# Attention's scores and transpositions over four PSUM banks, its outputs over one

## The chip, the cores and the metric

The kernel runs on one core of one Trainium2 chip, in one launch. The metric is the device time of that launch in microseconds (us): the median of three runs, with the lowest and the highest beside it.

## The reference, cut to what matters

Two layers (DEPTH = 2) of a hybrid mixer over 512 tokens of width 1024. Each layer normalises x, multiplies it with one wide input matrix, runs two branches beside each other and multiplies their concatenation with an output matrix. One branch is a gated linear recurrence (HGRN2, 8 heads of 128). The other, which the change touches, is sliding-window attention with 16 query heads of 64, two key/value heads and a learned sink per head:

```python
def sliding_window_attention(q, k, v, sinks):
    ...
    s = jnp.einsum('bnqkgd,bnskd->bnkgqs', qb, kw).astype(jnp.float32) * ATT_SCALE
    ...
    s = jnp.where(mask[None, :, None, None, :, :], s, NEG_INF)
    ...
    p = jax.nn.softmax(jnp.concatenate([s, sink], axis=-1), axis=-1)[..., :-1]
    o = jnp.einsum('bnkgqs,bnskd->bnqkgd', p.astype(v.dtype), vw)
    return o.reshape(B, S, KV * G * D)
...
    y = jnp.einsum('bse,ed->bsd', jnp.concatenate([o_h, o_a], axis=-1), w_out)
    return x + rms_norm(y, g_post)
```

A query block of 128 sees its own block of keys (up to the diagonal) and the block before it (past the diagonal).

## The kernel before

**The large products.** Every projection is cut into units of one PSUM bank (128 x 512). `step()` issues three matmuls of a unit (all on L284: high by high, high by low, low by high part of float32 operands that were split into two float32r parts); two units take turns. Weights come by DMA into `raw`, ACT casts the high part `whi` (L178) and DVE subtracts to get `wlo` (L179). Finished units are read out of PSUM by ACT or DVE.

**The attention.** `att_stream` (L613) is woven into the projections by `merge`, about one attention piece for a few L284 steps. A layer has 16 attention steps, numbered 0 to 15 here: four groups g of four heads, and for each the four query blocks n. A step with n = 0 sees one key block, the others two. Step i has three pieces on PE, which stand in the stream at different times:

- **S**, the scores (`att_scores`, L530): one bank with 8 matmuls (L541) where n = 0; else two banks with 4 matmuls each (L552). DVE masks them in PSUM (L544, or L556), takes the maximum (L545 or L557) and makes the negated maximum (`negm`, L560). Then ACT reads the bank and takes four exponentials (L566, two for each bank where there are two), POOL divides by the sum (L573). A score bank is free when its last exponential has been read.
- **T**, the transposition of the probabilities (`att_transpose`, L576), two steps later: one bank, 4 transposes (L579). ACT casts it (L330), DVE subtracts (L331), and the bank is free; POOL then masks the two halves (L591).
- **U**, the output (`att_value`, L598), four steps later: one bank, 2 or 4 matmuls of 128x512 (L605). ACT copies its upper half to the tile `u` (L607), of which there is one buffer; DVE adds the halves into `oa` in two instructions (L611), and the bank is free.

**The banks.** PSUM has 8 banks. Three are the units' (`pj`). Three, `sc0` to `sc2`, turn through `sc()`: scores, transpositions, and in other stages the norms' transpositions and the recurrence's products. Two are `ac`, taken in turn for U and, after the attention, for two products of the recurrence (L768, L779).

**What sets the order.** PE takes its instructions in program order, and so do DVE, ACT and POOL. The matmuls of attention and recurrence are pinned to the order in which they are written; a scheduler places everything else around them by its own model of times, and puts a wait in front of the instruction that needs a bank which is still being read. An instruction that waits on PE holds back all that stand behind it.

Of the kernel before, what the change touches and what calls it, by code (L numbers as in the profile page):

```python
# [10 lines left out]
F32 = mybir.dt.float32  # L11
# [29 lines left out]
PJ, SC = 3, 3  # L41
# [28 lines left out]
def hybrid_kernel(ctx: ExitStack, tc: tile.TileContext, x, wkv, win, wout, g_pre, g_post, lbp, ghead, sinks,  # L70
                  gcol_c, cos_f, sin_f, cos_t, sin_t, masks_c, out):
    nc = tc.nc
    P = 128
# [6 lines left out]
    ps = ctx.enter_context(tc.tile_pool(name="ps", bufs=2, space=bass.MemoryType.PSUM))  # L80
    dr = ctx.enter_context(tc.tile_pool(name="dr", bufs=1, space=bass.MemoryType.DRAM))

    def pin(ins):
        return tc.keep_in_program_order(ins)
# [2 lines left out]
        return ps.tile([P, 512], F32, tag="pj", name="pj", bufs=PJ)  # L87

    sc_tiles = [ps.tile([P, 512], F32, tag=f"sc{i}", name=f"sc{i}", bufs=1) for i in range(SC)]
    sc_turn = [0]  # L90

    def sc():
        sc_turn[0] += 1
        return sc_tiles[sc_turn[0] % SC]

    def ac():
        return ps.tile([P, 512], F32, tag="ac", name="ac", bufs=8 - PJ - SC)

    def tmp(tag, dt=F32, n=1):

        t = tp.tile([P, n, 512] if n > 1 else [P, 512], dt, tag=tag, name=tag, bufs=TB[tag])
        return t
# [25 lines left out]
    for l in range(1, DEPTH):  # L128
        i = plan_order.index((l, "kv"))
# [199 lines left out]
    def split_psum(hi, lo, src):  # L329
        nc.scalar.copy(hi, src)  # L330
        nc.vector.tensor_tensor(lo, src, hi.bitcast(F32), op=ALU.subtract)  # L331
# [96 lines left out]
    def layer(l, last):  # L428
# [101 lines left out]
        def att_scores(g, n):  # L530
            v = g // 2
            q = qs[g]
            hs = slice(4 * g, 4 * g + 4)
            t_ = slice(n * P, (n + 1) * P)
            mx_ = sm.tile([P, 4], F32, tag="mx", name="mx")
            cur = []
            if n == 0:
                S = sc()
                for h in range(4):
                    for p in range(2):  # L540
                        pin(nc.tensor.matmul(S[:, h * P:(h + 1) * P], lhsT=q[:, h, t_], rhs=kst[v][p][:, 0:P],  # L541
                                         start=(h == 0 and p == 0), stop=(h == 3 and p == 1)))
                Sv = S.rearrange("p (h s) -> p h s", h=4)
                nc.vector.copy_predicated(Sv, am4, neg.unsqueeze(2).broadcast_to([P, 4, P]))  # L544
                nc.vector.tensor_reduce(mx_, Sv, axis=AX.X, op=ALU.max)  # L545
                cur = [Sv[:, h, :] for h in range(4)]
            else:
                for hp_ in range(2):
                    S = sc()
                    for h in range(2):  # L550
                        for p in range(2):
                            pin(nc.tensor.matmul(S[:, h * 256:(h + 1) * 256], lhsT=q[:, 2 * hp_ + h, t_],  # L552
                                             rhs=kst[v][p][:, (n - 1) * P:(n + 1) * P],
                                             start=(h == 0 and p == 0), stop=(h == 1 and p == 1)))
                    Sv = S.rearrange("p (h s) -> p h s", h=2)
                    nc.vector.copy_predicated(Sv[:, :, P:2 * P], am2, Sv[:, :, 0:P])  # L556
                    nc.vector.tensor_reduce(mx_[:, 2 * hp_:2 * hp_ + 2], Sv[:, :, P:2 * P], axis=AX.X, op=ALU.max)  # L557
                    cur += [Sv[:, h, P:2 * P] for h in range(2)]
            negm = sm.tile([P, 4], F32, tag="negm", name="negm")
            nc.vector.scalar_tensor_tensor(negm, mx_, -SCALE, nsnk[:, l, hs], op0=ALU.mult, op1=ALU.min)  # L560
            ds_ = sm.tile([P, 4], F32, tag="ds", name="ds")
            nc.vector.tensor_tensor(ds_, snk[:, l, hs], negm, op=ALU.add)
            pt = tmp("s")
            sums = sm.tile([P, 4], F32, tag="sums", name="sums")
            for h in range(4):
                nc.scalar.activation(pt[:, h * P:(h + 1) * P], cur[h], AF.Exp, bias=negm[:, h:h + 1], scale=SCALE,  # L566
                                     accum_out=sums[:, h:h + 1])
            es = sm.tile([P, 4], F32, tag="es", name="es")
            nc.scalar.activation(es, ds_, AF.Exp)
            nc.vector.tensor_tensor(sums, sums, es, op=ALU.add)  # L570
            nc.vector.reciprocal(sums, sums)
            pv = pt.rearrange("p (h s) -> p h s", h=4)
            nc.gpsimd.tensor_tensor(pv, pv, sums.unsqueeze(2).broadcast_to([P, 4, P]), op=ALU.mult)  # L573
            return pt

        def att_transpose(g, n, pt, odd):  # L576
            T = sc()
            for h in range(4):
                pin(nc.tensor.transpose(T[:, h * P:(h + 1) * P], pt[:, h * P:(h + 1) * P], ident))  # L579
            tt_ = tmp("a", F32R, 2)  # L580
            split_psum(tt_[:, 0], tt_[:, 1], T)
            if n == 0:
                return [(n, tt_[:, 0]), (n, tt_[:, 1])]
            terms = []
            for which in range(2):
                if which == 0:
                    d = big.tile([P, 2, 512], F32R, tag="oy", name="pcur", bufs=6) if odd else tmp("b", F32R, 2)
                else:
                    d = big.tile([P, 2, 512], F32R, tag="q", name="pprev", bufs=QB)
                sg = -1 if which == 0 else 1  # L590
                nc.gpsimd.affine_select(out=d.rearrange("p a (h t) -> p (a h) t", h=4),  # L591
                                        in_=tt_.bitcast(F32).rearrange("p a (h t) -> p (a h) t", h=4),
                                        pattern=[[0, 8], [-sg, P]], compare_op=ALU.is_ge, fill=0.0,
                                        base=-which, channel_multiplier=sg)
                terms += [(n - which, d[:, 0]), (n - which, d[:, 1])]
            return terms

        def att_value(g, n, terms):  # L598
            v = g // 2
            t_ = slice(n * P, (n + 1) * P)  # L600
            if g == len(oa):
                oa.append(big.tile([P, 2, 512], F32, tag="oy", name="oa", bufs=6))
            U = ac()
            for i, (blk, d) in enumerate(terms):
                pin(nc.tensor.matmul(U, lhsT=vst[v][:, blk, :], rhs=d, start=(i == 0), stop=(i == len(terms) - 1)))  # L605
            ul = tmp("u")
            nc.scalar.copy(ul[0:64, :], U[64:128, :])  # L607
            Uv = U.rearrange("p (a b t) -> p a b t", a=2, b=2)
            lv = ul.rearrange("p (a b t) -> p a b t", a=2, b=2)
            for b in range(2):  # L610
                nc.vector.tensor_tensor(oa[g][64 * b:64 * b + 64, :, t_], Uv[0:64, :, b, :], lv[0:64, :, b, :], op=ALU.add)  # L611
# [60 lines left out]
        def hgrn(a):  # L672
# [94 lines left out]
            for j, f, k, q, A in hs:  # L767
                SU = ac()  # L768
                for n in range(NT - 1):
                    pin(nc.tensor.matmul(SU[:, n * P:(n + 1) * P], lhsT=kps[j][:, n * P:(n + 1) * P], rhs=vs(j, n), start=True, stop=True))  # L770
                st = sm.tile([P, 3, P], F32, tag="st", name="st", bufs=2)
                nc.scalar.copy(st[:, 0], SU[:, 0:P])
                for n in range(1, NT - 1):
                    nc.vector.scalar_tensor_tensor(st[:, n], st[:, n - 1], tots[j][:, n:n + 1], SU[:, n * P:(n + 1) * P],
                                                   op0=ALU.mult, op1=ALU.add)
                sts.append(st)
                yield 1.5
# [38 lines left out]
        def zh_stream(s):  # L816
            def evac(tt, o):
# [9 lines left out]
                def rest():  # L827
                    T = sc()
                    for j in range(4):
                        pin(nc.tensor.transpose(T[:, j * P:(j + 1) * P], g[:, j * P:(j + 1) * P], ident))  # L830
                    Tv = T.rearrange("p (j t) -> p j t", j=4)
                    nc.scalar.activation(hi[:, :, t_], Tv, AF.Copy, scale=gh[:, l:l + 1])
                    nc.vector.scalar_tensor_tensor(lo[:, :, t_], Tv, gh[:, l:l + 1], hi[:, :, t_].bitcast(F32), op0=ALU.mult, op1=ALU.subtract)
# [241 lines left out]
def _tables():  # L1075
# [3 lines left out]
    c, s = np.cos(ang).astype(np.float32), np.sin(ang).astype(np.float32)  # L1079
    cf = np.ascontiguousarray(np.tile(c.T, (4, 1)))  # L1080
    sf = np.ascontiguousarray(np.tile(s.T, (4, 1)))
# [48 lines left out]
```

## Time and profile before

| | before |
|---|---|
| median of 3 runs | 927.55 us |
| lowest, highest | 927.0, 927.8 us |
| the profiled execution's own time | 927.92 us |
| its span, first to last instruction | 926.2 us |
| PE busy | 908.4 us, 98% |
| DVE, ACT, POOL busy | 672.1, 462.5, 268.8 us |
| granted TensorE clock | 0.999 |

A matmul's busy time in the profile runs from its start to its modelled end, and consecutive ones overlap. How long PE really takes for a piece is therefore read from start to start. The attention of layer 0 lies at about 59 to 171 us, that of layer 1 at about 516 to 628 us.

### The profile page before, as it was taken

How to read it: one execution, taken by the hardware profiler on the slowest of the kernel's cores; microseconds unless marked ns; L12 is line 12 of the kernel's file. 1: busy time of each engine (PE TensorE's matmuls, PEld its weight loads, DVE VectorE, ACT ScalarE, POOL GpSimd, SP SyncE). 2: the span in 40 equal slices, each digit the busy share in tenths (PEclk: the TensorE clock that was granted, in tenths of full speed). 3: DMA queues.
4: the chain of work that ended last, by engine and by line, in shares of the span. 5: the costliest groups of instructions: out<-in, count | busy, mean ns of one | idle time of the engine just before them, and what ended most of it. 6: DMA issues, size and time to landing. Idle time of an engine off the chain costs nothing.

```text
span 926.2 us, 18985 instructions
## 1 busy us (share of the span) xinstructions
PE 908.4 (98%) x7240; PEld 751.1 (81%) x7240; DVE 672.1 (73%) x1326; ACT 462.5 (50%) x1100; POOL 268.8 (29%) x286
## 2 busy tenths in 40 slices
PE   8999999999999999999989999999999999999996
PEld 6888887878888888788878878888787887888885
DVE  5968977885766783955786689878867577748556
ACT  5535767536364451444453466674554636325242
POOL 3425443242221311311332254441323203113102
PEclk9999999999999999999999999999999999999999
DMA  6684612322222242423356555122223223323213
GB/s 223 187 234 135 171 36 80 92 82 80 70 86 94 64 136 69 138 70 112 117 160 178 162 148 171 58 69 92 70 80 99 62 81 114 104 70 94 91 35 136
DMA packets 56570, 100.74 MB, mean 109 GB/s; under 512 B 6560, under 2 KB 9120, under 8 KB 56480
## 3 DMA queue, kind: packets, MB, share of 16 engines
q1 hardware_dynamic: 56192, 99.40, 35.8%
q8 instruction: 57, 0.93, 0.4%
q14 instruction: 33, 0.27, 0.1%
q10 hardware_dynamic: 288, 0.14, 0.1%
HBM read 86.93 MB, written 12.58 MB: 107 GB/s over the span
## 4 chain that ended last, share of the span: by engine, by line
PE 85%; DVE 8%; ACT 3%; issue 2%; POOL 1%; DMA 0%; POOLq 0%; DVEq 0%; SPq 0%; ACTq 0%
PE pj L284 71%; PE sc L713 2%; PE sc L552 2%; PE ac L605 2%; DVE wlo L179 2%; PE ac L782 2%; PE ac L785 1%; PE ac L770 1%; ACT s L566 1%; PE sc L579 1%; PE sc L830 1%; DVE mx L557 1%; POOL r L345 1%; DVE a L331 1%; PE sc L760 1%
## 5 line engine op out<-in xcount | busy, mean ns | idle before, releaser
L284 PE MATMUL pj<-hhi,wlo 128*128 128x512 f32 x512 | 205.3, 401 | 0.0
L179 DVE TENSOR_TENSOR wlo<-raw,whi 128x512 fp32r<-128x512 f32 x249 | 182.5, 746 | 27.1 <-ACT whi L178 26.2
L284 PE MATMUL pj<-hhi,whi 128*128 128x512 f32 x512 | 200.0, 391 | 0.0
L284 PE MATMUL pj<-hlo,whi 128*128 128x512 f32 x512 | 199.7, 390 | 0.0
L178 ACT CAST whi<-raw 128x512 fp32r<-128x512 f32 x256 | 155.0, 621 | 84.1 <-PE pj L284 71.5
L284 PE MATMUL pj<-whi,ops 128*128 128x512 f32 (+1 forms) x520 | 173.5, 395 | 0.0
L284 PEld LDWEIGHTS pj<-whi,ops 128*128 128x128 f32 x520 | 97.2, 188 | 19.6
L284 PEld LDWEIGHTS pj<-hhi,whi 128*128 128x128 f32 x512 | 96.1, 188 | 20.9
L284 PEld LDWEIGHTS pj<-hhi,wlo 128*128 128x128 f32 x512 | 96.2, 188 | 19.2
L284 PEld LDWEIGHTS pj<-hlo,whi 128*128 128x128 f32 x512 | 96.3, 188 | 18.3
L284 PE MATMUL pj<-whi,hlo 128*128 128x512 f32 x256 | 103.5, 405 | 0.0
L284 PE MATMUL pj<-wlo,hhi 128*128 128x512 f32 x256 | 100.4, 392 | 0.3 <-DVE wlo L179 0.2
L284 PE MATMUL pj<-wlo,ops 128*128 128x512 f32 (+1 forms) x260 | 100.5, 387 | 0.0
L284 PE MATMUL pj<-whi,hhi 128*128 128x512 f32 x256 | 100.3, 392 | 0.0
L731 POOL TENSOR_TENSOR k<-k,tot 128x256 f32<-128x256 f32 x80 | 64.9, 830 | 108.7 <-PE sc L713 61.2
L566 ACT ACTIVATE s<-sc,negm 128x128 f32<-128x128 f32 x128 | 45.5, 368 | 38.6 <-DVE negm L560 38.6
L730 DVE TENSOR_TENSOR q<-q,tot 128x256 f32<-128x256 f32 x80 | 51.3, 673 | 14.5 <-PE sc L713 9.5
L284 PEld LDWEIGHTS pj<-whi,hhi 128*128 128x128 f32 x256 | 48.1, 188 | 10.2
L284 PEld LDWEIGHTS pj<-wlo,ops 128*128 128x128 f32 x260 | 49.0, 188 | 8.7
L284 PEld LDWEIGHTS pj<-wlo,hhi 128*128 128x128 f32 x256 | 48.3, 189 | 8.9 <-DVE wlo L179 1.0
L284 PEld LDWEIGHTS pj<-whi,hlo 128*128 128x128 f32 x256 | 48.2, 188 | 8.0
L681 DVE RECIPROCAL a<-f 128x256 f32<-128x256 f32 x16 | 28.0, 1750 | 28.4 <-ACT f L658 26.1
(185 smaller groups left out, 1423.8 us busy)
## 6 DMA issues: line engine op xcount, KB each, us to landing
raw<-in_win_dram SPq DMA_DIRECT2D x192, 256.0 KB, 2.7
raw<-in_wout_dram SPq DMA_DIRECT2D x64, 256.0 KB, 2.7
stack<-rot SPq DMA_DIRECT2D x16, 512.0 KB, 3.5
qs<-stack SPq DMA_DIRECT2D x32, 256.0 KB, 4.5
a<-in_x_dram SPq DMA_DIRECT2D x12, 256.0 KB, 3.2
raw<-in_wkv_dram SPq DMA_DIRECT2D x8, 256.0 KB, 3.6
x_mid<-a SPq DMA_DIRECT2D x8, 256.0 KB, 2.2
a<-x_mid SPq DMA_DIRECT2D x8, 256.0 KB, 3.1
```

The lines of the kernel that those rows point to most:

```text
L178: keep(nc.scalar.copy(hi, v))
L179: keep((nc.gpsimd if i in on_pool and i % 2 else nc.vector).tensor_tensor(lo, v, hi.bitcast(F32), op=ALU.subtract))
L284: nc.tensor.matmul(u.o, lhsT=u.sta(k, u.w)[i], rhs=u.mov(k, u.w)[j], start=(n == 0), stop=(n == len(u.list) - 1))
L331: nc.vector.tensor_tensor(lo, src, hi.bitcast(F32), op=ALU.subtract)
L552: pin(nc.tensor.matmul(S[:, h * 256:(h + 1) * 256], lhsT=q[:, 2 * hp_ + h, t_], rhs=kst[v][p][:, (n - 1) * P:(n + 1) * P], start=(h == 0 a ...
L566: nc.scalar.activation(pt[:, h * P:(h + 1) * P], cur[h], AF.Exp, bias=negm[:, h:h + 1], scale=SCALE, accum_out=sums[:, h:h + 1])
L605: pin(nc.tensor.matmul(U, lhsT=vst[v][:, blk, :], rhs=d, start=(i == 0), stop=(i == len(terms) - 1)))
L681: nc.vector.reciprocal(re, f2[:, :, 1])
L713: pin(nc.tensor.matmul(L[32 * b:32 * b + 32, c:c + 16], lhsT=k[:, o_:o_ + 32], rhs=qv[:, blk:blk + qu, 1, :], start=True, stop=True, tile_ ...
L730: nc.vector.tensor_tensor(qv[:, :, 1, :], qv[:, :, 1, :], tv[:, :, 0].unsqueeze(2).broadcast_to([P, nb, hh]), op=ALU.mult)
L731: nc.gpsimd.tensor_tensor(kv_[:, :, 0, :], kv_[:, :, 0, :], tv[:, :, 1].unsqueeze(2).broadcast_to([P, nb, hh]), op=ALU.mult)
L782: pin(nc.tensor.matmul(O[:, c], lhsT=A[:, c], rhs=vs(j, n), start=(n == 0), stop=False))
```

## The change

The two `ac` banks get names, `ac0` and `ac1`, and are handed out by a counter of their own. A new function `at()` turns over four banks, `sc0`, `sc1`, `sc2` and `ac0`, with the counter of `sc()`; scores and transpositions of the attention take their banks from it. The outputs U always take `ac1`. Everything else keeps `sc()` and `ac()`. No instruction is added or removed and no operand changes its size.

```diff
     sc_tiles = [ps.tile([P, 512], F32, tag=f"sc{i}", name=f"sc{i}", bufs=1) for i in range(SC)]
-    sc_turn = [0]
+    ac_tiles = [ps.tile([P, 512], F32, tag=f"ac{i}", name=f"ac{i}", bufs=1) for i in range(8 - PJ - SC)]
+    sc_turn, ac_turn = [0], [0]
...
     def ac():
-        return ps.tile([P, 512], F32, tag="ac", name="ac", bufs=8 - PJ - SC)
+        ac_turn[0] += 1
+        return ac_tiles[ac_turn[0] % len(ac_tiles)]
+
+
+    def at():
+        sc_turn[0] += 1
+        return (sc_tiles + ac_tiles[:1])[sc_turn[0] % (SC + 1)]
...
             if n == 0:
-                S = sc()
+                S = at()
...
                 for hp_ in range(2):
-                    S = sc()
+                    S = at()
...
         def att_transpose(g, n, pt, odd):
-            T = sc()
+            T = at()
...
-            U = ac()
+            U = ac_tiles[1]
```

The changed kernel's lines from L96 on stand 7 further down than those of before (L284 becomes L291, L605 becomes L612). The order of PE's instructions is the same but for a few places. In what follows a name such as `sc_79` is one bank's tile (`sc_78` to `sc_80` are `sc0` to `sc2`, `ac_81` and `ac_82` are `ac0` and `ac1`).

PE, layer 0, steps 1 to 4. Before, from the transposition T1 to the scores S4 and the transposition T2 (14 unit matmuls L284 stand between T1 and the first matmul of U0, L605):

```order
L579 MATMUL sc_79<-ident,s 128x128 x4
L284 MATMUL pj<-whi,hlo 128x512
...
L284 MATMUL pj<-whi,hhi 128x512
L605 MATMUL ac<-a,vst 128x512
L541 MATMUL sc_80<-kst,qs 128x128 x8
L579 MATMUL sc_78<-ident,s 128x128 x4
L605 MATMUL ac<-a,vst 128x512
```

The same place in the changed kernel:

```order
L586 MATMUL ac_81<-ident,s 128x128 x4
L291 MATMUL pj<-whi,hlo 128x512
L291 MATMUL pj<-wlo,hhi 128x512
L291 MATMUL pj<-whi,hhi 128x512
L548 MATMUL sc_78<-kst,qs 128x128 x8
L291 MATMUL pj<-wlo,hhi 128x512
...
L586 MATMUL sc_79<-ident,s 128x128 x4
```

S4 has moved up past 11 unit matmuls and stands 3 behind T1; T2 stands 5 unit matmuls behind S4, and U0 (both of its matmuls together) 6 behind T2. T2's bank is the one that the first half of S3 had. In layer 1 this place is unchanged. In both layers S8 also moves up, by 7 unit matmuls, and the second half of S9 no longer stands 2 unit matmuls behind the first; DVE's masks and ACT's exponentials of S4 and S8 move forward with them.

PE, the end of the attention in both layers, U13 to U15. Before, U13 (`pcur`, `pprev`), the first unit matmuls behind it, and U14 (`b`, `pprev`), which stands 9 unit matmuls behind U13:

```order
L605 MATMUL ac<-pcur,vst 128x512 x2
L605 MATMUL ac<-pprev,vst 128x512 x2
L284 MATMUL pj<-hhi,wlo 128x512
...
L605 MATMUL ac<-b,vst 128x512 x2
L605 MATMUL ac<-pprev,vst 128x512 x2
```

In the changed kernel U14 and what follows it up to U15:

```order
L612 MATMUL ac_82<-b,vst 128x512 x2
L612 MATMUL ac_82<-pprev,vst 128x512 x2
L291 MATMUL pj<-hlo,whi 128x512
L291 MATMUL pj<-hhi,whi 128x512
L291 MATMUL pj<-hhi,wlo 128x512
...
L612 MATMUL ac_82<-pcur,vst 128x512 x2
L612 MATMUL ac_82<-pprev,vst 128x512 x2
```

U14 now stands 19 unit matmuls behind U13, and U15 stands 7 behind U14, where it stood 15 behind.

DVE, the end of the attention in both layers, where the recurrence's first instructions (L681, L683, L685) stand among the last sums `oa`. Before:

```order
L681 RECIPROCAL a<-f 128x256 x2
L611 TENSOR_TENSOR oa<-ac,u 64x2x128 x2
L179 TENSOR_TENSOR wlo<-raw,whi 128x512 x2
L611 TENSOR_TENSOR oa<-ac,u 64x2x128 x2
L685 TENSOR_TENSOR b<-k,a 128x256
L683 TENSOR_TENSOR b<-q,f 128x256
L611 TENSOR_TENSOR oa<-ac,u 64x2x128 x2
```

And in the changed kernel:

```order
L688 RECIPROCAL a<-f 128x256 x2
L618 TENSOR_TENSOR oa<-ac_82,u 64x2x128 x2
L186 TENSOR_TENSOR wlo<-raw,whi 128x512 x2
L692 TENSOR_TENSOR b<-k,a 128x256
L618 TENSOR_TENSOR oa<-ac_82,u 64x2x128 x2
L690 TENSOR_TENSOR b<-q,f 128x256
L618 TENSOR_TENSOR oa<-ac_82,u 64x2x128 x2
```

The three pairs of `oa` are those of steps 13, 14 and 15; the pair of step 14 has gone behind L685 (now L692).

## Rows read from the trace of the kernel before

**Rows 1.** The page, its part on the engines: busy time, share of the span and instructions of each.

```profile
PE 908.4 (98%) x7240; PEld 751.1 (81%) x7240; DVE 672.1 (73%) x1326; ACT 462.5 (50%) x1100; POOL 268.8 (29%) x286
```

**Rows 2.** The waits of PE's weight loads over the whole run: who waited for what, then us in total, times, longest.

```profile
PEld sc L552 <- ACT s L566: 7.3, 16, 1.2
PEld sc L541 <- ACT s L566: 1.1, 3, 0.4
```

**Rows 3.** The timeline of PE in layer 0 at six places: start in us, duration in us, engine, line, operation, tiles, shapes, count, idle time before it and what ended it. The places are S7 (nothing waits), S8 and T6, the second half of S9, S10, S14, S15; ahead of and behind the pieces stand the unit matmuls next to them.

```profile
99.23 1.11 PE L552 MATMUL sc<-kst,qs 128*128 128x256 f32 x8
100.18 0.40 PE L284 MATMUL pj<-whi,hlo 128*128 128x512 f32 x1
...
106.37 0.39 PE L284 MATMUL pj<-whi,hlo 128*128 128x512 f32 x1
106.72 1.11 PE L541 MATMUL sc<-kst,qs 128*128 128x128 f32 x8
107.98 0.63 PE L579 MATMUL sc<-ident,s 128*128 128x128 f32 x4 [0.16 <-issue]
...
112.14 0.40 PE L284 MATMUL pj<-wlo,hhi 128*128 128x512 f32 x1
112.73 0.74 PE L552 MATMUL sc<-kst,qs 128*128 128x256 f32 x4 [0.19 <-ACT s L566]
113.31 0.39 PE L284 MATMUL pj<-whi,hhi 128*128 128x512 f32 x1
...
117.43 0.39 PE L284 MATMUL pj<-whi,hhi 128*128 128x512 f32 x1
118.89 0.40 PE L284 MATMUL pj<-whi,hlo 128*128 128x512 f32 x1
...
141.62 0.39 PE L284 MATMUL pj<-hhi,whi 128*128 128x512 f32 x1
142.79 1.44 PE L552 MATMUL sc<-kst,qs 128*128 128x256 f32 x8 [0.79 <-ACT s L566]
144.07 0.40 PE L284 MATMUL pj<-whi,hlo 128*128 128x512 f32 x1
...
148.62 0.39 PE L284 MATMUL pj<-hhi,whi 128*128 128x512 f32 x1
150.36 0.39 PE L284 MATMUL pj<-hhi,wlo 128*128 128x512 f32 x1
```

**Rows 4.** The timeline of PE in layer 1, the unit matmuls ahead of S5 and behind it (the two halves of S5 stand between them).

```profile
542.41 0.39 PE L284 MATMUL pj<-whi,hhi 128*128 128x512 f32 x1
544.46 0.39 PE L284 MATMUL pj<-whi,hlo 128*128 128x512 f32 x1
```

**Rows 5.** The timeline of PE and ACT in layer 0 at T1, the third unit matmul behind it, and the second of the four exponentials of step 3.

```profile
79.51 0.60 PE L579 MATMUL sc<-ident,s 128*128 128x128 f32 x4
80.81 0.40 PE L284 MATMUL pj<-whi,hhi 128*128 128x512 f32 x1
83.35 0.36 ACT L566 ACTIVATE s<-sc,negm 128x128 f32<-128x128 f32 x1
```

**Rows 6.** The timelines of the engines in layer 0 from step 12 to 15, in order of time: DVE masks S12; the second DVE sum of U8; U9's first matmuls; the second exponential of step 13; the two sums of U9; U10's first matmuls; the second exponential of step 14.

```profile
131.17 0.75 DVE L544 COPY_PREDICATED_SCALAR sc<-masks,neg 128x512 f32 x1 [0.41 <-PE sc L541]
139.09 0.42 DVE L611 TENSOR_TENSOR oa<-ac,u 64x256 f32<-64x256 f32 x1
139.56 0.62 PE L605 MATMUL ac<-pcur,vst 128*128 128x512 f32 x2
142.29 0.36 ACT L566 ACTIVATE s<-sc,negm 128x128 f32<-128x128 f32 x1
144.96 0.83 DVE L611 TENSOR_TENSOR oa<-ac,u 64x256 f32<-64x256 f32 x2
146.56 0.62 PE L605 MATMUL ac<-b,vst 128*128 128x512 f32 x2
148.57 0.36 ACT L566 ACTIVATE s<-sc,negm 128x128 f32<-128x128 f32 x1
```

**Rows 7.** The timelines at the end of the attention of layer 0, in order of time: U13's and U14's first matmuls on PE, the second reciprocal of the recurrence on DVE, the sums of U13, ACT's copy of U14, two `wlo`, the sums of U14.

```profile
162.73 0.62 PE L605 MATMUL ac<-pcur,vst 128*128 128x512 f32 x2
165.68 0.62 PE L605 MATMUL ac<-b,vst 128*128 128x512 f32 x2
167.10 1.75 DVE L681 RECIPROCAL a<-f 128x256 f32<-128x256 f32 x1 [1.18 <-POOL pprev L591]
168.76 0.78 DVE L611 TENSOR_TENSOR oa<-ac,u 64x256 f32<-64x256 f32 x2
169.66 0.58 ACT L607 COPY u<-ac 64x512 f32<-64x512 f32 x1 [2.59 <-DVE oa L611]
169.58 1.29 DVE L179 TENSOR_TENSOR wlo<-raw,whi 128x512 fp32r<-128x512 f32 x2
170.79 0.84 DVE L611 TENSOR_TENSOR oa<-ac,u 64x256 f32<-64x256 f32 x2
```

**Rows 8.** The timelines at the end of the attention of layer 1: U13's first matmuls, its sums.

```profile
619.29 0.62 PE L605 MATMUL ac<-pcur,vst 128*128 128x512 f32 x2
625.32 0.78 DVE L611 TENSOR_TENSOR oa<-ac,u 64x256 f32<-64x256 f32 x2
```

**Rows 9.** Busy time in 13 us of layer 0's attention: PE, PEld, DVE, ACT, POOL, each with its count, then the granted clock (PEclk), the DMA share and GB/s.

```profile
135.00:148.00 13.00, 12.21 (x65) 9.98 (x64) 12.55 (x25) 9.26 (x26) 6.75 (x6) 1.00 0.31 92
```

## The prediction, made before the changed kernel ran

> **What bounds the kernel now.** I read the page's engine line first: PE is busy for 908.4 of the span [rows 1], so DVE, ACT and POOL cost time only where PE stands still for them. PE takes its instructions in order; a stall there is added to the end, and one removed is taken off it, unless PE meets another wait a little later. Next come the waits of PE's weight loads: in 16 + 3 cases they wait for the exponentials L566, 7.3 + 1.1 = 8.4 us together [rows 2]. That is the score banks: a bank of `sc` is asked for again while ACT has not yet read it. It is also the most that four banks can give back. Last I read the timeline at these places, from start to start. S7 shows the undisturbed price of eight score matmuls: 100.18 - 99.23 = 0.95. Unit matmuls follow each other by 0.227: U13 (4) and 9 unit matmuls are 13 starts in 165.68 - 162.73 = 2.95 [rows 3, 7].
>
> **What the score waits cost, place by place (layer 0).** What exceeds 0.23 for the unit matmul ahead plus the undisturbed piece is the wait [rows 3].
> - S8 and T6: S8 starts 0.35 after its neighbour, 0.12 too late; T6 starts 1.26 after S8, 0.31 too late. 0.43.
> - S9, second half: 112.73 - 112.14 - 0.23 = 0.36, and 0.58 instead of 0.47 inside it. 0.47.
> - S10: 1.46 - 1.18 = 0.28.
> - S14: 144.07 - 141.62 - 1.18 = 1.27.
> - S15: 1.74 - 1.18 = 0.56.
>
> Together 3.0. Layer 1 runs the same order from S8 on, so I take 3.0 for it too, and 2.05 - 1.18 = 0.87 for S5 [rows 4]. Sum 6.9, inside the 8.4.
>
> **What of it comes back.** With four banks a piece asks for the bank of the piece four before it, not three. Three places are short even then. PE starts 0.14 after a bank's last exponential: 142.29 + 0.36 = 142.65, and S14 at 142.79 [rows 3, 6].
> - T2 in layer 0. S4 has moved up, T2 with it, and T2's bank is that of S3's first half, free at 83.35 + 0.36 = 83.71. Now PE is there at 80.81 + 0.23 + 0.95 (S4) + 5 x 0.23 = 83.1 to 83.2, and waits until 83.85 [rows 5]: 0.65. The start of step 3's exponentials does not move, since nothing ahead of them has. I count 0.6.
> - S14 and S15, both layers. The first half of S14 finds its bank free at 141.85; the second half wants that of S13's first half, which ACT leaves at 142.65, so it starts at 142.79 and not at 142.31; before it started some 0.7 later. U10 then stands at 146.56 - 0.7 = 145.86 and needs U9's sums: 144.96 + 0.83 + 0.14 = 145.93, another 0.07. S15's second half comes at about 148.68 and needs S14's first half: 148.57 + 0.36 + 0.14 = 149.07 [rows 3, 6]. Of 1.83 a layer, 0.7 remains, **1.1 is returned**. Here I take DVE and ACT to be where they were relative to PE; if they move forward, up to 1.1 a layer more is left.
>
> Score side: layer 0 0.43 + 0.47 + 0.28 + 0.7 - 0.6 = 1.3; layer 1 0.87 + 0.43 + 0.47 + 0.28 + 0.7 = 2.75. Gain **4.0**; bounds 3.4 (half a microsecond more of T2's kind) and 6.9.
>
> **What the outputs pay.** With one bank U(i) waits until DVE has made both sums of U(i-1). From step 1 to 13 the margin is there, thinnest at U9: U8's second sum ends at 139.09 + 0.42 = 139.51, and U9 starts at 139.56 [rows 6]. At the end of the attention it is not. U13's sums stand behind the recurrence's second reciprocal (167.10, itself held by POOL's masking of T15) and end at 168.76 + 0.78 = 169.54. In the new order U14 stands 4 + 19 starts behind U13's first: 162.73 + 23 x 0.227 = 167.95. It waits until 169.54 + 0.14 = 169.68: **1.73** [rows 7]. The chain to that reciprocal starts at T15, ahead of U13 on PE, so it shifts with PE and the wait stays. Behind the wait stand all later unit matmuls; nothing covers it. Then U15: U14's last matmul ends at about 170.75, ACT copies (0.58), DVE sums (0.84), so U15 may start at 172.4; 7 unit matmuls behind U14 it arrives at 169.68 + 11 x 0.227 = 172.2: 0.2 more. Layer 1 has the same spacing: 625.32 + 0.78 + 0.14 - (619.29 + 23 x 0.227) = 1.73 [rows 8]. Loss 2 x 1.95 = **3.9**. Bounds: nothing, if DVE came to U13's sums 1.7 earlier; 5, with half a microsecond more at U15, where POOL and DVE durations vary most (a `wlo` pair takes 1.29 in rows 7).
>
> DVE's step of L685 (now L692) ahead of U14's sums costs nothing: those sums now wait for ACT's copy at 171.4, after it. The recurrence's own use of `ac0` and `ac1` begins long after the attention and alternates as before. No instruction is added.
>
> **Sum.** 927.92 (the profiled execution) - 4.0 + 3.9 = 927.8. That execution stood 0.37 above the median, so the median becomes **927.4**.
>
> **The rivals.**
> 1. *The score gain stays whole.* DVE and ACT move forward with PE, S14 and S15 keep their 1.83 a layer, and T2 finds its bank free: 6.9 - 3.9 = 3.0 off, **924.5**. For it: DVE waited 0.41 for S12 at 131.17 [rows 6], so the chain to S14 does hang on PE. Against it: from 135 to 148 DVE is busy for 12.55 of 13 [rows 9]; there it has nothing to be faster with.
> 2. *The outputs follow DVE (slower).* If the sums do not come earlier when PE does, all that was gained ahead of step 9 is paid back at U9, whose margin is 139.56 - 139.51 = 0.05: layer 0 loses its 0.43 + 0.47 + 0.28 - 0.6 = 0.6 and layer 1 its 2.05. Only 0.7 a layer is left, against 3.9: 1.4 - 3.9, that is 2.5 more, **930.0**. It decides from the point where U8's sums move forward by less than U9 does. For it: DVE's 12.55 of 13. Against it: the 0.41 at 131.17, again. This is what the Trainium skill would expect (Perfetto Trace Analysis, Optimizing Tensor Performance, Matmuls: independent matmul groups should rotate through different banks, so that one's read-out overlaps the next one's matmuls). The trace bears it out at U14 and U15, where the next output comes before the sums, and not at the steps with a margin.
> 3. *The end does not wait.* U13's sums come before PE reaches U14: only the 4.0 counts, **923.4**. Against it: DVE's order still has both reciprocals ahead of these sums.
>
> That the change does not do what it says is excluded: the new order names the banks.
>
> **How the numbers follow.** Forecast 0.52, rival 1 0.25, rival 2 0.18, rival 3 0.05. 0.2% is 1.86 us, about what a measurement of this kernel can tell from no change: 925.7 and 929.4 are the borders. Rival 1 and 3 lie below the lower one, rival 2 above the upper; the forecast's own bounds put a little on either side. Faster 0.29, same 0.52, slower 0.19. The range takes in rivals 1 and 2 with half a microsecond beyond each: 924.0 to 930.4; outside lie rival 3 and the farther halves of the other two.
>
> **What would show it.** In the new profile: PE's waits for L566 fall from 8.4 to about 3 and stand at T2 of layer 0 and the second halves of S14 and S15; a new wait for the sums (L618) stands at U14, 1.7 us in each layer, with a short one at U15; none over 0.2 at U1 to U13. A wait over 0.5 at U9 makes rival 2 right, none at S14 and S15 rival 1, none at U14 rival 3. I am wrong in the working, whatever the time, if scores still wait in S8 to S10, or if PE meets new waits for `wlo` or for a unit's bank.

## The result, and the profile after

The changed kernel took 931.42 us (median of five runs, 929.77 to 931.99) against 927.32 us for the kernel before (927.0 to 927.8): a ratio of 1.0037, 95% interval 1.0024 to 1.0050. It is slower, and the time lies 1.0 us above the upper end of the predicted range. The five runs are of two kinds. Two took 929.77 and 929.86 us at a mean granted clock of 0.999 and 0.998; the other three took 931.42, 931.99 and 931.83 us at 0.997, 0.995 and 0.995. The profiled execution is the one of 929.77 us, with a span of 927.7 us. The loss therefore has two parts: 1.85 us against the profiled execution before, which the trace shows, and some 2 us more in the longer runs, which it does not.

The page of the changed kernel, the line of the engines:

```profile
PE 908.2 (98%) x7240; PEld 751.1 (81%) x7240; DVE 666.7 (72%) x1326; ACT 461.5 (50%) x1100; POOL 267.8 (29%) x286
```

PE's work is what it was [rows 1]; only its stops have moved. The waits over the whole run, of PE and of its weight loads (who waited for what, us in total, times, longest):

```profile
PE ac L612 <- DVE oa L618: 4.3, 2, 2.1
PE sc L586 <- ACT s L573: 0.7, 1, 0.7
PEld sc L559 <- ACT s L573: 1.0, 3, 0.3
PEld ac L559 <- ACT s L573: 0.3, 1, 0.3
```

The weight loads' 8.4 us of waits for exponentials [rows 2] are down to 1.0 + 0.3 = 1.3; with the wait of 0.7 that stands with PE it is 2.0. In their place stands a wait for the sums, once in each layer. The timeline of PE from U13 to U15 in layer 0 shows it, and U14 in layer 1:

```profile
160.96 0.61 PE L612 MATMUL ac<-pcur,vst 128*128 128x512 f32 x2
...
165.95 0.39 PE L291 MATMUL pj<-hhi,wlo 128*128 128x512 f32 x1
168.46 0.70 PE L612 MATMUL ac<-b,vst 128*128 128x512 f32 x2 [2.12 <-DVE oa L618]
...
170.84 0.39 PE L291 MATMUL pj<-hlo,whi 128*128 128x512 f32 x1
171.31 0.70 PE L612 MATMUL ac<-pcur,vst 128*128 128x512 f32 x2
...
625.37 0.70 PE L612 MATMUL ac<-b,vst 128*128 128x512 f32 x2 [2.14 <-DVE oa L618]
```

From the last unit matmul to U14 it is 168.46 - 165.95 = 2.51, of which 0.23 is that matmul: a stop of 2.28, where 1.73 was predicted. U15 comes 171.31 - 170.84 - 0.23 = 0.24 late.

To set all kernels beside each other I read two distances on PE in each layer: from the first score matmul S0 to U13 (the attention, where the scores' waits lie) and from U13 to the recurrence's first matmul (L700 before, L707 now; the tail, where the outputs' waits lie). The stretches from there to the next layer and to the end agree within 0.4 us in all traces; S0 itself starts between 58.8 and 59.6, without a pattern.

| profiled execution (us) | attention, layer 0 | tail, layer 0 | attention, layer 1 | tail, layer 1 | time, clock |
|---|---|---|---|---|---|
| before | 103.46 | 23.90 | 103.25 | 23.89 | 927.92, 0.999 |
| changed | 102.16 | 26.65 | 100.82 | 26.65 | 929.77, 0.999 |
| changed, again (e3) | 102.18 | 27.92 | 100.90 | 27.90 | 932.42, 0.995 |
| outputs alone (e2) | 103.46 | 26.13 | 103.22 | 26.20 | 932.05, 0.998 |
| outputs alone, again (e9) | 103.47 | 26.13 | 103.28 | 26.08 | 932.11, 0.999 |
| U14 in `ac0` (e1) | 102.15 | 24.22 | 100.86 | 24.25 | 925.47, 0.998 |
| one tile of reciprocals (e4) | 102.16 | 25.32 | 100.86 | 25.34 | 927.17, 0.998 |
| U14 in `ac0`, layer 1 only (e5) | 102.16 | 26.65 | 100.90 | 24.25 | 927.57, 0.998 |
| a reciprocal more (e6) | 102.17 | 27.88 | 100.85 | 27.92 | 932.43, 0.995 |
| e1, e4 and T2 in `ac1` (e7) | 103.13 | 23.89 | 100.86 | 23.89 | 925.16, 0.999 |
| e1 and e4 (e8) | 102.13 | 23.90 | 100.86 | 23.89 | 924.48, 0.998 |
| e8 and two banks exchanged (e10) | 101.94 | 23.89 | 100.88 | 23.89 | 924.12, 0.998 |

The changed kernel gains 1.30 + 2.43 = 3.73 in the attention and pays 2.75 + 2.76 = 5.51 in the tails: 1.78 net, of the 1.85.

### The profile page after: what moved, and what is told of

It is laid out like the page before. It is cut to its first block, busy times and chain, and to the rows that moved or that the text cites. A ratio compares the mean times of both kernels' runs of the same rounds, so it can differ in the third digit from the quotient of the medians.

```text
span 927.7 us, 18979 instructions
## 1 busy us (share of the span) xinstructions
PE 908.2 (98%) x7240; PEld 751.1 (81%) x7240; DVE 666.7 (72%) x1326; ACT 461.5 (50%) x1100; POOL 267.8 (29%) x286
## 4 chain that ended last, share of the span: by engine, by line
PE 86%; DVE 6%; ACT 3%; POOL 2%; issue 2%; DMA 0%; POOLq 0%; DVEq 0%; ACTq 0%
PE pj L291 70%; PE sc L720 2%; PE ac L612 2%; PE ac L789 2%; PE sc L559 1%; PE ac L792 1%; PE ac L777 1%; DVE wlo L186 1%; PE sc L586 1%; PE sc L837 1%; ACT s L573 1%; DVE mx L564 1%; POOL r L352 1%; PE sc L767 1%; DVE a L913 1%
## 5 line engine op out<-in xcount | busy, mean ns | idle before, releaser
L291 PE MATMUL pj<-hhi,wlo 128*128 128x512 f32 x512 | 205.2, 401 | 0.0
L291 PE MATMUL pj<-hhi,whi 128*128 128x512 f32 x512 | 200.0, 391 | 0.0
L291 PE MATMUL pj<-hlo,whi 128*128 128x512 f32 x512 | 199.7, 390 | 0.0
L291 PE MATMUL pj<-whi,ops 128*128 128x512 f32 (+1 forms) x520 | 173.5, 395 | 0.0
L291 PEld LDWEIGHTS pj<-whi,ops 128*128 128x128 f32 x520 | 97.2, 188 | 19.7
L291 PEld LDWEIGHTS pj<-hhi,whi 128*128 128x128 f32 x512 | 96.1, 188 | 20.9
L291 PEld LDWEIGHTS pj<-hhi,wlo 128*128 128x128 f32 x512 | 96.2, 188 | 19.2
L291 PEld LDWEIGHTS pj<-hlo,whi 128*128 128x128 f32 x512 | 96.3, 188 | 18.4
L291 PE MATMUL pj<-whi,hlo 128*128 128x512 f32 x256 | 104.0, 407 | 0.0
L291 PE MATMUL pj<-wlo,hhi 128*128 128x512 f32 x256 | 100.3, 392 | 0.3 <-DVE wlo L186 0.2
L291 PE MATMUL pj<-wlo,ops 128*128 128x512 f32 (+1 forms) x260 | 100.5, 387 | 0.0
L291 PE MATMUL pj<-whi,hhi 128*128 128x512 f32 x256 | 100.3, 392 | 0.0
L291 PEld LDWEIGHTS pj<-whi,hhi 128*128 128x128 f32 x256 | 48.0, 188 | 10.4
L291 PEld LDWEIGHTS pj<-wlo,ops 128*128 128x128 f32 x260 | 49.0, 188 | 8.7
L291 PEld LDWEIGHTS pj<-wlo,hhi 128*128 128x128 f32 x256 | 48.3, 189 | 8.7 <-DVE wlo L186 1.0
L291 PEld LDWEIGHTS pj<-whi,hlo 128*128 128x128 f32 x256 | 48.2, 188 | 7.8
L573 ACT ACTIVATE s<-sc,negm 128x128 f32<-128x128 f32 x96 | 34.2, 367 | 37.5 <-DVE negm L567 37.4
```

What stands on the lines that cost most here:

```text
L291: nc.tensor.matmul(u.o, lhsT=u.sta(k, u.w)[i], rhs=u.mov(k, u.w)[j], start=(n == 0), stop=(n == len(u.list) - 1))
```

## The experiments

Theory ahead of them: the scores' gain is real, the stop at U14 eats it, and the same stop is what lets the clock fall in some executions. Rivals: the gain was never there; the stop waits for something else than the predicted chain; the spread of the runs has nothing to do with the stop. All kernels start from the changed one, and each diff is against it.

**e1: the tail's stop alone taken away.**

```diff
-            U = ac_tiles[1]
+            U = ac_tiles[0 if (g, n) == (3, 2) else 1]
```

> Only the output of step 14 goes back to the bank that the outputs lost (ac0), the other fifteen stay in ac1. Theory (the waits of the scores were saved, and the stops ahead of U14 and U15 at the end of the attention eat the gain): U14 starts where PE reaches it, so about 2.28 us per layer of the stop ahead of U14 and up to 0.24 ahead of U15 go, 4.6 to 5.1 us in all; an execution at a granted clock of 0.999 then takes 929.8 - 5 = 924.7 us (924.3 to 925.3). If the stop at U14 is also what lets the granted clock of an execution fall to 0.995 to 0.997, all runs show 0.998 or more and lie within 1 us of each other. Rival (the spread of the changed kernel's runs has nothing to do with the stop): the runs still spread over 2 us, with clocks down to 0.995, and the median is near 926.3. Second rival (the gain of the scores was never there): about 927.5, as before.

925.05 us (924.29 to 925.47, five runs) against 928.13 before: ratio 0.9963 [0.9950, 0.9975]. PE from U13 to U15 in layer 0:

```profile
161.79 0.62 PE L612 MATMUL ac<-pcur,vst 128*128 128x512 f32 x2
...
164.74 0.62 PE L612 MATMUL ac<-b,vst 128*128 128x512 f32 x2
...
169.28 0.70 PE L612 MATMUL ac<-pcur,vst 128*128 128x512 f32 x2
```

U14 follows U13 as closely as in the kernel before [rows 7], the attention keeps its gain, and all five runs show 0.998 or 0.999 and lie within 1.2 us of each other (1 was expected). The tails' remaining 0.3 over the kernel before is U15, which still comes 0.23 late. One bank for one output in each layer turns a loss into a gain. That the gain was never there is refuted.

**e2 and e9: the outputs' half of the change alone**, measured twice.

```diff
-        return (sc_tiles + ac_tiles[:1])[sc_turn[0] % (SC + 1)]
+        return sc_tiles[sc_turn[0] % SC]
```

> Half of the change alone: all outputs in ac1, scores and transpositions over three banks as before. Theory: the score waits are those of the kernel before, and the stop at the end of the attention alone is added: U14 waits about 1.7 to 2.0 us per layer and U15 0.2, so an execution at a clock of 0.999 takes 927.9 + 4 = 931.9 us (931 to 932.5), and if the stop lets the clock fall, some runs show 0.995 to 0.997 and are 1.6 to 2.2 us longer. Rival (the four banks of the scores bring nothing, and one bank for the outputs costs what the whole change costs): 929.8 at a clock of 0.999, as the changed kernel's own.

> The kernel with all outputs in ac1 and the scores over three banks again, unaltered: its stops at U14 are 1.75 and 1.82 us, against 2.28 and 2.30 in the changed kernel. Theory (the granted clock falls behind a stop of TensorE only where it is as long as the changed kernel's): all runs at 0.997 or more and within 1.5 us of each other, median 932.2. Rival (any stop at that place may let the clock fall): some runs at 0.995, 2 to 2.5 us longer.

932.24 us (931.90 to 933.06) against 928.13, and 932.62 us (931.78 to 933.27) against 928.24; ratios 1.0044 [1.0031, 1.0058] and 1.0047 [1.0034, 1.0059]. The two U14 in the first trace:

```profile
169.47 0.70 PE L612 MATMUL ac<-b,vst 128*128 128x512 f32 x2 [1.60 <-DVE oa L618]
...
628.24 0.70 PE L612 MATMUL ac<-b,vst 128*128 128x512 f32 x2 [1.66 <-DVE oa L618]
```

Counted from start to start the stops are 1.75 and 1.82 (1.74 and 1.74 in e9): the predicted 1.73, now that PE stands where it stood before. All ten runs show clocks of 0.997 or more.

**e3: the changed kernel again.** No edit.

> The changed kernel again, unaltered, for the spread of its runs. Theory: runs near 929.8 at a clock of 0.998 or 0.999 and runs near 931.7 at 0.995 to 0.997, and where the profiled execution is one of the second kind, the granted clock is seen at half right behind the stop at U14 (after 166 us or after 623 us). Rival: the clock falls at another place, or the longer runs show a clock of 0.998 or more and are longer for another reason.

930.74 us (929.72 to 932.52, ten runs) against 928.13: ratio 1.0030 [1.0021, 1.0039]. Six runs took 929.7 to 931.0 at 0.998 or 0.999, four took 932.15 to 932.52 at 0.993 to 0.995. This time the profiled execution is of the second kind. PE in four stretches (us, busy time with its count, granted clock, DMA share, GB/s):

```profile
166.00:169.90 3.90, 1.77 (x9) 1.00 0.00 0
169.90:173.40 3.50, 3.50 (x10) 0.51 0.51 155
...
624.00:627.30 3.30, 1.17 (x5) 1.00 0.00 0
627.30:630.80 3.50, 3.50 (x10) 0.51 0.40 150
```

The same stretch of the changed kernel's first trace, and two unit matmuls of the second trace within it:

```profile
169.90:173.40 3.50, 3.42 (x15) 1.00 0.44 155
```

```profile
170.13 0.63 PE L291 MATMUL pj<-hhi,whi 128*128 128x512 f32 x1
170.56 0.63 PE L291 MATMUL pj<-hhi,wlo 128*128 128x512 f32 x1
```

Right behind the stop at U14 the granted clock is at 0.51 for a stretch, nearly all of it the lower level of 1.2 GHz. Unit matmuls follow each other by 0.43 in place of 0.23, and ten matmuls are seen where fifteen were. It happens in both layers and nowhere else but at the program's end. Against the first trace the tails are 1.27 and 1.25 longer (table), 2.5 of the 2.65 us between the two executions. That is net: PE comes to U15 later here, and U15's stop of 0.24 is gone, so a fall by itself takes more than the tails show.

**e4: the chain ahead of the sums made shorter.** Both reciprocals of a pair write one tile, so that the second no longer waits for POOL's select.

```diff
-            qbs, kbs, tots = [], [], []
+            qbs, kbs, tots, ra = [], [], [], halves("a")[0]
...
-                re = halves("a")[0][:, 0:256]
+                re = ra[:, 256 * j:256 * j + 256]
```

> In the recurrence the two reciprocals of a pair write the two halves of one tile, in place of two tiles of which the second is still read by GpSimd's select of step 15; nothing else is altered. Theory (U14 waits for sums 13, which stand in VectorE's order behind the second reciprocal, which waits for that select): the second reciprocal follows the first at once, 1.2 us earlier, sums 13 end near 167.1 in place of 168.31, the stop at U14 is 1.1 us (was 2.28) in each layer, and the time is 2.0 to 2.4 us less than the changed kernel's at the same clock, 927.5. Rival (U14 waits for something else that ends at the same time, such as ScalarE's copy or the select itself): the stop stays at 2.2 to 2.3 us and the time is 929.8.

927.12 us (926.67 to 928.51, eleven runs), ratio 0.9989 [0.9981, 0.9998]. DVE and PE in layer 0:

```profile
163.22 3.35 DVE L688 RECIPROCAL a<-f 128x256 f32<-128x256 f32 x2
166.49 0.78 DVE L618 TENSOR_TENSOR oa<-ac,u 64x256 f32<-64x256 f32 x2
167.42 0.70 PE L612 MATMUL ac<-b,vst 128*128 128x512 f32 x2 [0.81 <-DVE oa L618]
```

The two reciprocals now stand together, the sums come 1.3 earlier relative to U13 (5.26 behind it, not 6.57), the stop at U14 is 0.97, and both tails are 1.3 shorter. The chain select, second reciprocal, sums, U14 is shown. All eleven clocks are 0.997 or 0.998.

**e5: the stop taken away in layer 1 only.** The line of e1 with `l == 1` in its condition.

> The output of step 14 goes to the other bank in the second layer alone; the first layer keeps the stop ahead of U14. Theory (each layer's stop costs about 2.7 us by itself, and each may let the clock fall once, for 3.4 us at half, which costs 1.3 us): an execution at a clock of 0.998 or 0.999 takes 927.5 us, one with the one fall that is still possible shows 0.996 to 0.997 and takes 928.8, and the fall, where the profiled execution has it, stands near 170 us and none near 625 us. Rival (the falls come in pairs, or hang on something that both layers share): executions 2.4 us longer than the others at 0.995, or none longer at all.

928.00 us (927.08 to 928.65, eleven runs), ratio 0.9999 [0.9990, 1.0008]. U14 of both layers:

```profile
168.93 0.70 PE L612 MATMUL ac<-b,vst 128*128 128x512 f32 x2 [2.12 <-DVE oa L618]
...
621.30 0.62 PE L612 MATMUL ac<-b,vst 128*128 128x512 f32 x2
```

A layer's stop at U14 costs 2.4 us at full clock (26.65 against 24.25; U15's stop stays), whatever the other layer does; 2.7 was expected. On the falls this run is inconclusive: three of the eleven runs show 0.996 or 0.997 and are the longest (928.58 to 928.65), as one fall would make them, but eight others already reach up to 928.25, and the profiled execution had no fall.

**e6: the stop made longer.** In the first pair of the recurrence the second reciprocal is issued twice.

```diff
-                nc.vector.reciprocal(re, f2[:, :, 1])
+                [nc.vector.reciprocal(re, f2[:, :, 1]) for _ in range(2 if (a, j) == (0, 1) else 1)]
```

> The second reciprocal ahead of sums 13 is done twice (the same values into the same place), in both layers, so that the stop at U14 becomes 1.75 us longer, about 4.0 us; the work is otherwise the same. Theory (sums 13 stand behind that reciprocal and the whole of it is on the path; the clock falls behind a stop that is long enough): 3.5 us more than the changed kernel at the same clock, 933.3 us, and the falls near 171 us and 630 us come in most runs or all of them, which then take 935 to 936.5 us at 0.995. Rival (the falls have nothing to do with the length of the stop): falls in fewer than half of the runs, as before, and a median near 933.5.

929.97 us (929.10 to 932.43, eleven runs) against 927.92: ratio 1.0025 [1.0016, 1.0034]. The lever missed: the scheduler put the extra reciprocal behind the sums of U13.

```profile
166.23 1.75 DVE L688 RECIPROCAL a<-f 128x256 f32<-128x256 f32 x1 [1.18 <-POOL pprev L598]
167.90 0.78 DVE L618 TENSOR_TENSOR oa<-ac,u 64x256 f32<-64x256 f32 x2
170.26 1.75 DVE L688 RECIPROCAL a<-f 128x256 f32<-128x256 f32 x1
```

So the stop at U14 is 2.27 and 2.30 as in the changed kernel, and the run says nothing of longer stops. U15, which the scheduler set later too, does not stop here, so these tails compare with the changed kernel's only roughly. As a third sample of the same stop it counts: three of eleven runs are at 0.995 with 932.2 to 932.4 us, eight at 0.997 with 929.1 to 931.4, and the profiled execution, one of the three, has its clock at 0.51 in the same two stretches:

```profile
169.90:173.40 3.50, 3.50 (x10) 0.51 0.45 150
627.30:630.80 3.50, 3.50 (x10) 0.51 0.52 150
```

**e7: three stops taken away at once**: e1, e4, and T2 of layer 0 in `ac1`, which no output uses yet.

```diff
-            T = at()
+            T = [at(), ac_tiles[1]][(l, g, n) == (0, 0, 2)]
```

> The changed kernel with three of its stops taken away: the output of step 14 in ac0, one tile for the reciprocals of a pair, and in the first layer the transposition of step 2 in ac1, which no output uses yet. Theory: 925.05 us of the kernel with step 14 in ac0, less 0.24 us per layer (U15 no longer waits for sums 13, which end 1.2 us earlier) and less 0.6 to 0.85 us (the stop at T2): 923.7 us (923.0 to 924.5), at clocks of 0.998 or more in every run. Rival (ends that come earlier at these places are waited for at the next one, U0 behind T2's split above all): 925.0.

925.75 us (924.77 to 926.20, eight runs), ratio 0.9976 [0.9966, 0.9986]: the rival's mechanism is right, though its 925.0 was too low. PE, ACT and DVE around step 2:

```profile
83.04 0.60 PE L586 MATMUL ac<-ident,s 128*128 128x128 f32 x4
87.32 0.59 ACT L337 CAST a<-ac 128x512 fp32r<-128x512 f32 x1
87.95 0.69 DVE L338 TENSOR_TENSOR a<-ac,a 128x512 fp32r<-128x512 f32 x1
88.69 0.74 PE L612 MATMUL ac<-a,vst 128*128 128x512 f32 x2 [1.58 <-DVE a L338]
```

T2 no longer waits, but `ac1` now holds its result until ACT, in whose queue step 4's exponentials stand first, and DVE have read it. U0 needs the bank and, though the scheduler has set it later, in the middle of S5, stands idle for 1.58, where T2 stood idle for 0.69 in the changed kernel: the stop came back as a larger one (attention of layer 0: 103.13 against 102.15).

**e8: e1 and e4 without that third edit.**

> The changed kernel with the output of step 14 in ac0 and with one tile for the two reciprocals of a pair; the transposition of step 2 stays where the turn puts it. Theory: the kernel with step 14 in ac0 (925.05 us), less the 0.24 us per layer that U15 still waited there for sums 13: 924.6 us (924.2 to 925.1), clocks of 0.997 or more in every run; U0 no longer waits behind step 2's split, so the 1.58 us of the kernel with all three edits are not there. Rival (the three-edit kernel's 925.75 us came from the tile of the reciprocals, not from U0): 925.8.

924.63 us (924.47 to 924.88, five runs) against 928.24: ratio 0.9962 [0.9949, 0.9974]: the time that was expected, and the tile of the reciprocals is not what held e7 back. The tails are those of the kernel before to 0.01 us, so the whole tail loss is accounted for.

**e10: e8, and T2 exchanges its bank with the second half of S5 in layer 0.**

```diff
-    def at():
+    def at(k=0):
...
-        return (sc_tiles + ac_tiles[:1])[sc_turn[0] % (SC + 1)]
+        return (sc_tiles + ac_tiles[:1])[(sc_turn[0] + k) % (SC + 1)]
...
-                    S = at()
+                    S = at(2 * ((l, g, n, hp_) == (0, 1, 1, 1)))
...
-            T = at()
+            T = at(2 * ((l, g, n) == (0, 0, 2)))
```

> As the kernel with step 14 in ac0 and one tile for the reciprocals, and in the first layer the banks of two takers are exchanged: the transposition of step 2 takes the bank that the transposition of step 1 has left, and the second half of step 5's scores takes the one that step 3's exponentials still read when step 2 comes. Theory (T2 stops 0.85 us because its turn falls on the bank whose exponentials are running, not because its own data are late): the stop at 83 us goes, no other comes, 0.7 to 0.85 us less than that kernel: 923.8 us. Rival (U0 or T3 waits for what T2's earlier start doesn't hurry, as with ac1): no less than that kernel, 924.6.

924.12 us (923.92 to 925.48, five runs), ratio 0.9960 [0.9946, 0.9974]: the fastest, though its interval covers that of e8. PE and DVE at T2:

```profile
82.77 0.39 PE L291 MATMUL pj<-whi,hhi 128*128 128x512 f32 x1
83.56 0.63 PE L586 MATMUL ac<-ident,s 128*128 128x128 f32 x4 [0.40 <-DVE ds L569]
...
82.73 0.68 DVE L338 TENSOR_TENSOR a<-ac,a 128x512 fp32r<-128x512 f32 x1
```

The stop fell from 0.85 to 0.56, not to nothing. The releaser named is a small DVE step; the bank itself was held until 82.73 + 0.68 = 83.41 by DVE's part of T1's split, and T2 starts 0.15 after that. Both expectations were half right.

## Why the prediction was wrong, point by point

**The scores.** The waits for exponentials fell to 2.0 us, at the three kinds of places named: T2 of layer 0 and the second halves of S14 and S15; none is left at S8 to S10. T2 stops 0.85 (0.65 worked out, 0.6 counted). T2, S14 and S15 in layer 0:

```profile
82.38 0.39 PE L291 MATMUL pj<-whi,hhi 128*128 128x512 f32 x1
82.87 0.36 ACT L573 ACTIVATE s<-sc,negm 128x128 f32<-128x128 f32 x1
83.46 0.63 PE L586 MATMUL sc<-ident,s 128*128 128x128 f32 x4 [0.69 <-ACT s L573]
...
140.69 0.39 PE L291 MATMUL pj<-hhi,whi 128*128 128x512 f32 x1
142.26 0.39 PE L291 MATMUL pj<-whi,hlo 128*128 128x512 f32 x1
...
146.98 0.39 PE L291 MATMUL pj<-hhi,whi 128*128 128x512 f32 x1
148.54 0.39 PE L291 MATMUL pj<-hhi,wlo 128*128 128x512 f32 x1
```

S14 stands between the first pair of unit matmuls and S15 between the second: 142.26 - 140.69 - 1.18 = 0.39 and 148.54 - 146.98 - 1.18 = 0.38 are left of their waits. (The prediction wrote 1.1 for what is lost there again; its own three terms, 0.48, 0.07 and 0.39, add up to 0.94.)

From S0 to S12 PE gains 0.65 in layer 0, where 0.43 + 0.47 + 0.28 - 0.6 = 0.58 was predicted, and from there to U13 0.65, where 0.7 was: 1.30 in all. In layer 1 it is 1.73 and 0.70, 2.43 in place of 2.75, so what is missing is missing ahead of S12. Layer 0's sizes, which the prediction carried over, were not too large; but in layer 1 U1 and U5 start 0.14 and 0.15 behind the sums of the output before, 0.13 and 0.08 late: there the one bank is just waited for. 3.73 in place of 4.0: this step held.

Rival 1 (the whole gain stays) is out by S14 and S15. Rival 3 is out by U14. Rival 2 shows only in such small stops: the second sum of U8 and U9 stand 0.14 apart in layer 0,

```profile
137.98 0.42 DVE L618 TENSOR_TENSOR oa<-ac,u 64x256 f32<-64x256 f32 x1
138.54 0.70 PE L612 MATMUL ac<-pcur,vst 128*128 128x512 f32 x2
```

so U9's margin is used up, but no output before U14 starts as much as 0.2 late in either layer.

**The tail is the step that failed**: "The chain to that reciprocal starts at T15, ahead of U13 on PE, so it shifts with PE and the wait stays." The end of the chain is as told (e4), its start is not. T15 on PE, step 15's first exponential, and the cast of T14's split behind it on ACT, before:

```profile
153.85 0.37 ACT L566 ACTIVATE s<-sc,negm 128x128 f32<-128x128 f32 x1 [0.83 <-DVE negm L560]
159.75 0.58 ACT L330 CAST a<-sc 128x512 fp32r<-128x512 f32 x1
160.21 0.60 PE L579 MATMUL sc<-ident,s 128*128 128x128 f32 x4
```

and after, with step 13's second exponential, which answers to [rows 6], ahead of them, and with the second reciprocal and the sums of U13, which answer to [rows 7]:

```profile
141.18 0.36 ACT L573 ACTIVATE s<-sc,negm 128x128 f32<-128x128 f32 x1
...
152.61 0.37 ACT L573 ACTIVATE s<-sc,negm 128x128 f32<-128x128 f32 x1 [1.40 <-DVE negm L567]
158.51 0.58 ACT L337 CAST a<-sc 128x512 fp32r<-128x512 f32 x1
158.45 0.60 PE L586 MATMUL sc<-ident,s 128*128 128x128 f32 x4
...
165.85 1.75 DVE L688 RECIPROCAL a<-f 128x256 f32<-128x256 f32 x1 [1.18 <-POOL pprev L598]
167.53 0.78 DVE L618 TENSOR_TENSOR oa<-ac,u 64x256 f32<-64x256 f32 x2
```

T15 moved forward by 1.76 and U13 by 1.77. The exponentials, the cast, the reciprocal and the sums moved by 1.24, 1.24, 1.25 and 1.23. (Of each, 0.47 is the earlier start of S0 in this execution.) From step 15's exponentials on ACT has its own queue to work off (the copy of an output, a table load and four activations ahead of the cast), and the exponentials wait for DVE, the fuller engine in this part of the attention [rows 9]. So the chain starts at DVE and ACT, and followed PE for 1.23 of 1.77. The stop grew by the difference: 1.73 + 0.54 = 2.27, measured 2.28.

Up to step 13 the engines had moved alike: S12 on PE by 1.12 (130.13 to 129.01), step 13's second exponential by 1.11. So what PE gained behind it, at S14 and S15, came back almost whole as stop at U14. Layer 1 shows the same: U13 moved by 1.44, its sums by 0.88 (625.32 to 624.44), and 1.73 + 0.56 = 2.29, measured 2.30. That the chain starts at DVE and ACT is read from these rows; no run altered its start alone. e2 and e9 are the counter-check: where PE does not gain, the stop is 1.74 to 1.82.

The remainder of the tail's 2.75 is U15's 0.24 (0.2 predicted) and some 0.2 for restarting PE behind the stops. In all 5.5 in place of 3.9. The bound of 5 that the prediction gave was too low, and it was argued from U15, not from U14. Where it treats S14 and S15 the prediction takes DVE and ACT not to move forward with PE; for the tail it took the contrary. By its own figures the 0.7 that PE gains there would have made the stop 1.73 + 0.7 = 2.43.

With the two terms as measured the sum is 927.92 - 3.73 + 5.51 = 929.70; the profiled execution took 929.77. The tail's 1.6 more than forecast makes the change slower, but by itself it leaves the time inside the range.

**What was missing is a term for the clock.** The prediction priced the stop at its length. A stop of 2.28 us had a second price here: behind it the granted clock went to half in some executions, 1.27 and 1.25 us net in the two layers of e3's trace. With three longer runs of five the median went from 929.8 to 931.4, out of the range. The run of 931.42 us itself, at 0.997, has no trace; it may hold one fall, or none, for the kernel before spreads by 1.7 us (927.27 to 928.96) without a clock under 0.997. What supports the term: the two traces with falls (e3, e6) have them at U14 in both layers; and clocks of 0.995 or less were seen in 2 of 5, 4 of 10 and 3 of 11 runs of the three kernels with this stop in both layers, but in none of the 44 runs of e1, e2, e4, e7, e8, e9 and e10, and in none of the 53 runs of the kernel before beside them (0.997 and more). Of the 44, the 21 of e1, e2 and e4 ran on the chip of e3, and the 8 of e7 on that of e6; the chip of e8, e9 and e10 did not run the changed kernel. That the falls go with the stop is therefore shown, and that its length decides is not: only the five runs of e2 set a shorter stop of 1.75 and 1.82 us beside e3 on one chip.

On the clock the Trainium skill (TensorE: Matmul & The Clock Gate, A second HAM failure mode: psum-queue depth-cycling) tells of a kernel whose matmul groups cycle through PSUM banks and whose frequent short stops between groups send the clock down and up again. In the two traces here single stops of 2.3 us do this, one in each layer, and stops of 1.82 us or less were not seen to. Why some executions of one kernel fall and others do not stays open, and so does a longer stop, since e6 did not make one.

## What to carry to other kernels

When a PSUM bank goes from one user to another, look at the losing user where its stage ends: PE runs on into work of another kind there, and the read-out stands behind that work's VectorE and ScalarE steps. It may need its second bank for one output only (e1: 925.05 us in place of about 931). When a gain on PE is forecast, a wait that "moves along" must be followed back to the engine on which its chain really starts; one that starts on a full engine gets longer by what PE gains and that engine does not. A bank lent for a moment (e7) must be read out by its next user's turn, by the queues as they stand, not only be free when it is lent.

## What the hardware showed unexpectedly

A PE stop of 2.3 us in an otherwise full stream was followed, in a part of the runs, by a granted clock of 0.51 in place of 1.00 over the 3.5 us right behind it. Two traces show it, at both places; a mean clock as low as theirs was seen in 9 of 26 runs, these two among them. In e3 a fall cost 1.27 and 1.25 us net. At the same place no clock under 0.997 was seen with stops of 1.74 to 1.82 us (ten runs) or of 0.97 to 0.99 us (eleven).
